# A state-space model inside a transformer layer: its elementwise passes on GpSimd, small corner clears on VectorE, its stores and loads one step earlier

## The chip, the cores and the metric

The kernel runs on one core of one Trainium2 chip. The metric is the device time of one execution in microseconds, the median of the runs shown. The core has five engines with an instruction stream each: TensorE (PE, with its weight loads shown as PEld), VectorE (DVE), ScalarE (ACT), GpSimd (POOL) and SyncE (SP), which here only issues DMA transfers (SPq in the trace). An engine takes its instructions strictly in the order in which they stand in its stream; where one waits, those behind it wait too.

## The reference

One layer of a hybrid encoder, for a prompt of 1024 frames and a running stream of 32 further frames (1056 columns together), in float32:

```python
proj = x @ w_in                                   # columns for attention, SSM and RWKV
mla_out  = mla_mixer(q_lat, kv_lat, k_rope, ...)  # 6 heads, causal in chunks of 64
s5_out   = s5_mixer(u, x0, ...)                   # 16 groups x 16 channels, 64 complex states each
rwkv_out = rwkv_mixer(p_rwkv, ...)                # 6 heads x 64
x = layer_norm(ALPHA * x + concat(mla_out, s5_out, rwkv_out) @ w_out)
x = layer_norm(ALPHA * x + square(relu(x @ w_up)) @ w_down)
```

The attention masks by chunks, and so on the diagonal of a block of 128 keys by 128 queries one corner of 64 by 64 is zero:

```python
key_chunk = arange(s) // 64
mask = key_chunk[None, :] <= q_chunk[:, None]
p = softmax(where(mask, s, NEG_INF)); out = p @ v
```

The SSM is a complex diagonal recurrence per group, and a gated output:

```python
state_t = lam_bar * state_(t-1) + b_bar @ u_t     # complex, 64 states per group
y = real(c @ state) + d * u
z = gelu(y);  s5_out = z * sigmoid(z @ w_glu + b_glu)
```

## The kernel before

The program passes four stages: projections and the set-up of RWKV (to about 320 us), the mix stage with attention, SSM and RWKV side by side (to about 700 us), the output projection with the first layer norm (to about 760 us), and the MLP. The change touches the mix stage alone.

**Order.** Three Python generators issue that stage. `stage_mix` advances attention, and after its 50th step, at every seventh, the SSM by one step (`S5_FROM`, `S5_STEP`); `side_by_side` sets 2.5 of these steps against one step of the RWKV stream. This gives the order in which the code is issued. A list scheduler then sets the order on each engine by its own costs of the instructions, so a row that becomes cheaper, dearer or ready earlier in its reckoning can move on every engine. `issue_after(mark)` keeps what it encloses behind an instruction named, for the SSM's steps behind the last VectorE instruction of the RWKV stream (`g.scan_dve`).

**The SSM, `stage_s5`.** The 16 groups go in four passes `q` of four. What follows calls them the first to the fourth group. A group holds one tile `ces` of 128 x 4 x 536 (two planes of tables, then the planes `e` and `es`), with the 64 real and 64 imaginary parts of the state on the 128 partitions. Its steps, each ended by a `yield`:

- SP loads the inputs and the kernel matrix (`ut`) and the input matrix `em`, and the tables (`ces<-tab_d`). PE multiplies (`s5e`), ACT copies into `e` and, with the halves swapped, into `es`, for two groups a step.
- L643 and L644: both planes times the tables, then added. ACT fills `es` with the decay (L645, `ces<-rho`), POOL clears two columns of it (L646), VectorE scans along the row (L647, the recurrence), and ACT writes the scan's halves swapped into `es` (L649, two of 64 x 536).
- L651 and L652: both planes times the tables, then subtracted.
- PE multiplies out (`s5y`), ACT copies (`yo`, inside `ces`), two groups a step; after them SP stores `z_d` (L665).

`ut`, `em` and `ces` have one buffer each, so the next group's loads wait until the last one's readers are done. Behind the fourth group stand the final states (`so`, L672 and L673), sixteen loads of the whole result (`zt<-z_d`, L680) and the Gelu on ACT (L683), with a load of its function table before it and one back to the exponentials behind it.

**Attention, `attn_out`.** For each tile of 128 keys PE makes scores `st`, ACT the numerators `ptk` (L1280, an exponential), POOL clears the corner on the diagonal (L1282), and PE multiplies with the values (`av`, L1255). At the end of a block of queries ACT copies the sums (`po`) and inverts them (L1263, L1264), and VectorE finishes (L1265 to L1268: `rt`, `rec`, `ot`). Row maxima are taken on VectorE (L1226, `mx<-sc`).

**RWKV.** Of its block steps, the pieces named later are: `ld`, the loads; PE's products `pra` and its transposes `prt` with ACT's copy `r` (L841); `prb`; the products `prn` with ACT's copy into `r` (L869); `prw` with ACT's copies `wu` (L883); `prg`; `pru` with ACT's copies `yb` (L919) and VectorE's `gq` (L917); and the chain over the state, `pry` and `prs` on PE (L940, L944) and `st` on VectorE (L946, L947), where each step needs the last. All these products share three banks of PSUM (`pr`).

Of the kernel before, what the change touches and what calls it, by code (L numbers as in the profile page):

```python
# [11 lines left out]
ALU = mybir.AluOpType  # L12
# [61 lines left out]
def log_exp_table(g, users, keep=True):  # L74

    pre = g.nc.scalar.preload_act_table_set("natural_log_exp_and_others")
    for u in users:
        g.tc.add_manual_dep(pre.ins, u.ins.name, mybir.DependencyInfo(mybir.DependencyClass.NoSync, mybir.DependencyReason.DATA), reason="table")
    if keep:
        g.le = pre.ins  # L80
# [318 lines left out]
G5 = 16  # L399
# [7 lines left out]
def bc(ap, shape):  # L407
    return ap.broadcast_to(shape)
# [191 lines left out]
NG = 4  # L600
# [3 lines left out]
def stage_s5(g):  # L604

    nc = g.nc
    V = nc.vector
    sp = g.s5  # L610
    for q in range(G5 // NG):
        gs = slice(NG * q, NG * q + NG)
        ut = sp.tile([P, NY * L5], F32, tag="ut", name="ut", bufs=1)
        u = ut[:, :NG * NY].rearrange("p (g k) -> p g k", k=NY)
        tz = ut[:, NG * NY:NG * NY + NG * P].rearrange("p (g x) -> p g x", x=P)
        nc.gpsimd.memset(u[:, :, P:P + 1], 0.0)
        nc.gpsimd.memset(tz, 0.0)
        src = g.u_d[q // 2][64 * (q % 2):64 * (q % 2) + 64].rearrange("(g c) (t k) -> (c t) g k", c=16, t=L5)
        nc.sync.dma_start(out=u[:, :, 0:P], in_=src[:, :, 0:P])
        nc.sync.dma_start(out=u[:, :, P + 1:NY], in_=src[:, :, P:NC5])  # L620
        em = sp.tile([P, NG, P], F32, tag="em", name="em", bufs=1)
        nc.sync.dma_start(out=em, in_=g.em_d[:, gs])
        for s in range(8):
            nc.sync.dma_start(out=tz[s:P:L5, :, 16 * s:P], in_=g.kt_d[:, gs, 0:(8 - s) * 16])
        ces = g.rl.tile([P, 4, NG * NX], F32, tag="ces", name="ces", bufs=1)
        tb = ces.rearrange("p w (g k) -> p w g k", k=NX)
        e, es = tb[:, 2], tb[:, 3]
        nc.sync.dma_start(out=tb[:, 0:2], in_=g.tab_d[:, :, gs])

        for j in range(0, NG, 2):  # L630
            ps = g.psc.tile([P, 512], F32, tag="sc", name="s5e")[:, :2 * NY].rearrange("p (j k) -> p j k", k=NY)
            for i in range(2):
                nc.tensor.matmul(out=ps[:, i], lhsT=em[:, j + i], rhs=u[:, j + i], start=True, stop=True)
            nc.scalar.activation(out=e[:, j:j + 2, 1:NX], in_=ps, func=AF.Copy)
            for i in range(2):
                nc.scalar.activation(out=es[hsl(1 - i), j:j + 2, 1:NX], in_=ps[hsl(i)], func=AF.Copy)
            yield
        nc.gpsimd.memset(tb[:, 2:4, :, 0:1], 0.0)
        nc.gpsimd.tensor_copy(out=e[:, :, P + 1], in_=g.x0[:, 0, gs])
        cl = sp.tile([P, NG, P], F32, tag="em", name="cl", bufs=1)  # L640
        nc.sync.dma_start(out=cl, in_=g.cl_d[:, P * NG * q:P * NG * (q + 1)].rearrange("p (g x) -> p g x", x=P))

        V.tensor_tensor(out=ces[:, 2:4], in0=ces[:, 2:4], in1=ces[:, 0:2], op=ALU.mult)  # L643
        V.tensor_tensor(out=ces[:, 2], in0=ces[:, 2], in1=ces[:, 3], op=ALU.add)  # L644
        nc.scalar.activation(out=es, in_=bc(g.rho[:, gs, None], [P, NG, NX]), func=AF.Copy)  # L645
        nc.gpsimd.memset(es[:, :, 0:P + 2:P + 1], 0.0)  # L646
        V.tensor_tensor_scan(out=ces[:, 2], data0=ces[:, 3], data1=ces[:, 2], initial=0.0, op0=ALU.mult, op1=ALU.add)  # L647
        for i in range(2):
            nc.scalar.activation(out=ces[hsl(1 - i), 3], in_=ces[hsl(i), 2], func=AF.Copy)  # L649
        yield  # L650
        V.tensor_tensor(out=ces[:, 2:4], in0=ces[:, 2:4], in1=ces[:, 0:2], op=ALU.mult)  # L651
        V.tensor_tensor(out=ces[:, 2], in0=ces[:, 2], in1=ces[:, 3], op=ALU.subtract)  # L652
        yield
        for i, k in enumerate((P, NX - 1)):
            nc.gpsimd.tensor_copy(out=g.fin[:, i, gs], in_=e[:, :, k])

        yo = ces[:, 3, :NG * NY].rearrange("p (g k) -> p g k", k=NY)
        for j in range(0, NG, 2):
            ps = g.psc.tile([P, 512], F32, tag="sc", name="s5y")[:, :2 * NY].rearrange("p (j k) -> p j k", k=NY)
            for i in range(j, j + 2):  # L660
                nc.tensor.matmul(out=ps[:, i - j], lhsT=tz[:, i], rhs=u[:, i], start=True, stop=False)
                nc.tensor.matmul(out=ps[:, i - j], lhsT=cl[:, i], rhs=e[:, i, 0:NY], start=False, stop=True)
            nc.scalar.activation(out=yo[:, j:j + 2], in_=ps, func=AF.Copy)
            yield
        nc.sync.dma_start(out=g.z_d[gs].rearrange("g x k -> x g k"), in_=yo)  # L665

    so = sp.tile([P, NG, P], F32, tag="em", name="so", bufs=1).rearrange("p a b -> p (a b)")[0:G5, 0:256].rearrange("p (i s r) -> p i s r", i=2, r=2)
    ps = g.psc.tile([P, 4, P], F32, tag="sc", name="s5l")
    for i in range(2):
        nc.tensor.transpose(out=ps[0:16, i], in_=g.fin[:, i], identity=g.ident)  # L670
    for i in range(2):
        nc.scalar.activation(out=so[:, i], in_=ps[0:16, i].rearrange("p (r s) -> p s r", r=2), func=AF.Copy)  # L672
        nc.scalar.dma_start(out=g.o["s5_p" if i == 0 else "s5_s"], in_=so[:, i])  # L673
    yield

    zt = g.rl.tile([P, 4, NG * NX], F32, tag="ces", name="zt", bufs=1).rearrange("p a b -> p (a b)")[:, :2 * L5 * NY]
    zv = zt.rearrange("p (h t k) -> p h t k", h=2, t=L5)
    for h in range(2):
        for i in range(8):
            nc.sync.dma_start(out=zv[16 * i:16 * i + 16, h], in_=g.z_d[8 * h + i].rearrange("(t c) k -> c t k", c=16))  # L680
    wg = sp.tile([P, NG, P], F32, tag="em", name="wg", bufs=1).rearrange("p a b -> p (a b)").rearrange("p (k m) -> p k m", k=2)
    nc.sync.dma_start(out=wg, in_=g.a["w_glu"])
    log_exp_table(g, [nc.scalar.activation(out=zt, in_=zt, func=AF.Gelu_apprx_tanh)], False)  # L683
    yield
    yield
    for m in range(2):
        om = sp.tile([P, NY * L5], F32, tag="ut", name="ot", bufs=1)
        ot = om.rearrange("p (k t) -> p t k", t=L5)
        for t, n in ((0, 3), (3, 3), (6, 2)):
            ps = g.psc.tile([P, 512], F32, tag="sc", name="s5g")[:, :n * NY]  # L690
            for k in range(2):
                nc.tensor.matmul(out=ps, lhsT=wg[:, k, m * P:m * P + P], rhs=zt[:, (k * L5 + t) * NY:(k * L5 + t + n) * NY], start=k == 0, stop=k == 1)
            nc.scalar.activation(out=ot[:, t:t + n], in_=ps.rearrange("p (t k) -> p t k", k=NY), func=AF.Identity, bias=g.vec[:, V_BGLU + m:V_BGLU + m + 1])
            yield
        log_exp_table(g, [nc.scalar.activation(out=om, in_=om, func=AF.Sigmoid)], False)
        V.tensor_tensor(out=ot, in0=ot, in1=zv[:, m], op=ALU.mult)
        nc.sync.dma_start(out=g.mg_d[3 + m, :, 0:TP], in_=om[:, 0:TP])
        nc.sync.dma_start(out=g.mg_d[3 + m, :, TP:T], in_=om[:, TP + L5:TP + L5 + TS])
        yield
# [13 lines left out]
def hsl(i):  # L713
    return slice(64 * i, 64 * i + 64)
# [527 lines left out]
def attn_out(g, h, qh, ql, vo, ot):  # L1242

    nc = g.nc
# [27 lines left out]
    for s, n in ((0, 512), (TP, TS), (512, 512)):  # L1272
        tiles = range((s + n) // P) if n > TS else range(8, 13)
        for kt in tiles:
            c = max(0, kt * P - s) if n > TS else 0
            w = P if kt < 12 else TS
            ps = g.pst.tile([P, 512], F32, tag="st", name="st")
            mm3(nc, [ps[:w, c:n]], kh[:, kt * P:kt * P + w], kl[:, kt * P:kt * P + w], [(qh[:, s + c:s + n], ql[:, s + c:s + n])], True, True)
            pt = g.ap.tile([P, 512], F32, tag="ptk", name="ptk", bufs=g.npt)
            nc.scalar.activation(out=pt[:w, c:n], in_=ps[:w, c:n], func=AF.Exp, scale=MLA_SCALE)  # L1280
            if n > TS and kt * P >= s:
                nc.gpsimd.memset(pt[64:128, c:c + 64], 0.0)  # L1282
            yield
            if late:
                av(*late)
                yield
            late = s, n, kt, c, w, pt, tiles
# [583 lines left out]
```

## Time and profile before

| What | Value |
|---|---|
| Median of 3 runs | 1610.53 us (1609.14 to 1616.11) |
| The profiled execution | 1609.9 us, span 1608.1 us |
| Mean granted TensorE clock | 0.965 |
| Share of the span: PE, DVE, ACT, POOL | 93%, 57%, 32%, 26% |

The span runs from the first instruction to the last; what lies outside it belongs to the execution's time. Rows of the profile name an instruction by line, engine, operation and tile (output <- input). A row of one stretch begins with its bounds and its width in us, then has for PE, PEld, DVE, ACT and POOL in turn the busy time and in brackets the number of instructions, then the granted clock (1 is full speed), the DMA engines' busy share and GB/s. A row of one instruction begins with its start and its duration, both in us; "x16" at its end means that so many stand together, and a bracket says how long the engine stood still just before and for what. A row of waits has the total in us, the number of waits and the longest.

### The profile page before, as it was taken

The page shows a single profiled execution, that of the slowest core. Times are in us where ns is not written, and L with a number is a line of the kernel's source. Part 1 is how long each engine was busy: PE and PEld are TensorE (multiplying, and loading weights), DVE is VectorE, ACT ScalarE, POOL GpSimd, SP SyncE. Part 2 cuts the span into 40 slices and gives each one's busy share as a digit, 9 for nine tenths or more (in the row PEclk, how much of TensorE's full clock was granted, in tenths as well). Part 3 has the DMA queues.
Part 4 walks back from the last instruction along what each step waited for, and adds up shares of the span by engine and source line. Part 5 has one row for each costly group of instructions (what it writes and reads, how often), then busy time and mean ns, then how long its engine had stood idle before and what let it go on. Part 6 is the DMA issues. An engine that isn't in the chain of part 4 may idle for free. (4 is left out here: it accounts for less than half of the span.)

```text
span 1608.1 us, 26358 instructions
## 1 busy us (share of the span) xinstructions
PE 1487.7 (93%) x10855; PEld 1336.1 (83%) x10855; DVE 920.6 (57%) x1676; ACT 510.6 (32%) x991; POOL 415.9 (26%) x394
## 2 busy tenths in 40 slices
PE   7899898578899798888999999999999999999995
PEld 7889786466667566566879999999999999999995
DVE  8476959363566544453865755554454454545457
ACT  5344433314544545542323212222121112221122
POOL 4623663511121101211422221222121112221123
PEclk9999999788999999999999999999999999999998
DMA  5314471437233221233512111111111111111012
GB/s 183 132 59 175 148 191 31 115 87 127 71 86 87 63 75 42 72 98 92 174 56 79 40 40 41 52 53 49 44 43 50 40 40 53 53 40 53 14 41 82
DMA packets 112621, 123.50 MB, mean 77 GB/s; under 512 B 51280, under 2 KB 87812, under 8 KB 112120
## 3 DMA queue, kind: packets, MB, share of 16 engines
q1 hardware_dynamic: 92516, 102.53, 21.8%
q10 hardware_dynamic: 19632, 18.27, 3.8%
q8 instruction: 85, 1.39, 0.4%
q0 software_dynamic: 352, 1.01, 0.2%
q14 instruction: 36, 0.29, 0.1%
HBM read 89.05 MB, written 32.68 MB: 76 GB/s over the span
## 5 line engine op out<-in xcount | busy, mean ns | idle before, releaser
L63 PE MATMUL acc<-xh,uphi 128*128 128x384 f32 (+1 forms) x768 | 249.0, 324 | 0.0
L65 PE MATMUL acc<-xl,uphi 128*128 128x384 f32 (+1 forms) x768 | 248.1, 323 | 0.0
L67 PE MATMUL acc<-xh,uplo 128*128 128x384 f32 (+1 forms) x768 | 247.8, 323 | 0.0
L1538 DVE TENSOR_TENSOR rl<-rl 128x384 f32<-128x384 f32 (+1 forms) x96 | 142.2, 1481 | 176.2 <-ACT rl L1537 174.3
L1566 DVE TENSOR_TENSOR yacc<-yacc,acc 128x384 f32<-128x384 f32 (+2 forms) x344 | 158.9, 508 | 112.1 <-PE acc L67 112.0
L63 PE MATMUL acc<-hh,dnhi 128*128 128x384 f32 (+2 forms) x736 | 209.3, 320 | 0.0
L65 PE MATMUL acc<-hl,dnhi 128*128 128x384 f32 (+2 forms) x736 | 207.2, 320 | 0.0
L67 PE MATMUL acc<-hh,dnlo 128*128 128x384 f32 (+2 forms) x736 | 197.5, 319 | 0.0
L50 POOL TENSOR_TENSOR dnlo<-dnraw,dnhi 128x1024 fp32r<-128x1024 f32 x30 | 72.5, 2417 | 336.8 <-ACT dnhi L49 321.5
L63 PEld LDWEIGHTS acc<-xh,uphi 128*128 128x128 f32 x768 | 144.2, 188 | 0.2 <-ACT xh L49 0.2
L65 PEld LDWEIGHTS acc<-xl,uphi 128*128 128x128 f32 x768 | 144.3, 188 | 0.0
L67 PEld LDWEIGHTS acc<-xh,uplo 128*128 128x128 f32 x768 | 144.3, 188 | 0.0
L50 POOL TENSOR_TENSOR uplo<-upraw,uphi 128x1024 fp32r<-128x1024 f32 x34 | 81.6, 2401 | 238.3 <-ACT uphi L49 238.3
L63 PE MATMUL acc<-xh,wmhi 128*128 128x384 f32 (+3 forms) x384 | 131.9, 344 | 9.3 <-ACT xh L49 8.2
L65 PE MATMUL acc<-xl,wmhi 128*128 128x384 f32 (+3 forms) x384 | 130.2, 339 | 1.6 <-DVE xl L50 1.6
L63 PEld LDWEIGHTS acc<-hh,dnhi 128*128 128x128 f32 x736 | 131.6, 188 | 0.0
L65 PEld LDWEIGHTS acc<-hl,dnhi 128*128 128x128 f32 x736 | 131.5, 188 | 0.0
L67 PE MATMUL acc<-xh,wmlo 128*128 128x384 f32 (+3 forms) x384 | 129.6, 338 | 0.0
L67 PEld LDWEIGHTS acc<-hh,dnlo 128*128 128x128 f32 x736 | 128.9, 188 | 0.0
L49 ACT ACTIVATE dnhi<-dnraw 128x1024 fp32r<-128x1024 f32 x30 | 31.8, 1060 | 298.9 <-PE acc L65 249.2
L49 ACT ACTIVATE hh<-rl 128x384 fp32r<-128x384 f32 (+1 forms) x96 | 47.9, 499 | 148.7 <-DVE rl L1538 148.7
L63 PEld LDWEIGHTS acc<-xh,wmhi 128*128 128x128 f32 (+1 forms) x384 | 73.9, 192 | 12.8 <-ACT xh L49 8.5
(489 smaller groups left out, 2881.2 us busy)
## 6 DMA issues: line engine op xcount, KB each, us to landing
upraw<-in_w_up SPq DMA_DIRECT2D x32, 512.0 KB
dnraw<-in_w_dn SPq DMA_DIRECT2D x30, 512.0 KB
ld<-rw SPq DMA_DIRECT2D x24, 320.0 KB
wmraw<-in_w_m SPq DMA_DIRECT2D x12, 512.0 KB
wo<-in_w_out SPq DMA_DIRECT2D x8, 512.0 KB
z<-in_xa SPq DMA_DIRECT2D x8, 512.0 KB
out_y<-o SPq DMA_DIRECT2D x8, 512.0 KB
xr<-in_xt SPq DMA_DIRECT2D x8, 384.0 KB
```

What stands on the lines that cost most here:

```text
L49: nc.scalar.activation(out=hi, in_=ps, func=AF.Copy)
L50: (lo_eng or nc.vector).tensor_tensor(out=lo, in0=ps, in1=hi.bitcast(F32), op=ALU.subtract)
L63: nc.tensor.matmul(out=outs[i], lhsT=lh, rhs=rhs[i][0], start=start, stop=False)
L65: nc.tensor.matmul(out=outs[i], lhsT=lh, rhs=rhs[i][1], start=False, stop=False)
L67: nc.tensor.matmul(out=outs[i], lhsT=ll, rhs=rhs[i][0], start=False, stop=stop)
L1538: nc.vector.tensor_tensor(out=r[:, :n], in0=r[:, :n], in1=r[:, :n], op=ALU.mult)
L1566: nc.vector.tensor_tensor(out=y, in0=y, in1=ps[i][:, :n], op=ALU.add)
```

## The change

It has three parts. The line numbers of the mix stage grow by 5 to 8: L643 becomes L648, L645 L650, L649 L654, L651 L656, L665 L670, L683 L691, L841 L849, L1280 L1288.

- The four elementwise passes of each group, sixteen in all, go from VectorE to POOL. The scan stays on VectorE, the copies on ACT.
- The 48 clears of the numerators' corners go from POOL to VectorE.
- `z_d`'s store and the next group's loads of `ut` and `em` are issued in the step of the last output copy, where they were issued at the beginning of the next step. The load of the tables stays where it was.

```diff
@@ -608,7 +608,8 @@
     nc = g.nc
     V = nc.vector
     sp = g.s5
-    for q in range(G5 // NG):
+
+    def load(q):
         gs = slice(NG * q, NG * q + NG)
         ut = sp.tile([P, NY * L5], F32, tag="ut", name="ut", bufs=1)
         u = ut[:, :NG * NY].rearrange("p (g k) -> p g k", k=NY)
@@ -622,6 +623,10 @@
         nc.sync.dma_start(out=em, in_=g.em_d[:, gs])
         for s in range(8):
             nc.sync.dma_start(out=tz[s:P:L5, :, 16 * s:P], in_=g.kt_d[:, gs, 0:(8 - s) * 16])
+        return gs, ut, u, tz, em
+
+    gs, ut, u, tz, em = load(0)
+    for q in range(G5 // NG):
         ces = g.rl.tile([P, 4, NG * NX], F32, tag="ces", name="ces", bufs=1)
         tb = ces.rearrange("p w (g k) -> p w g k", k=NX)
         e, es = tb[:, 2], tb[:, 3]
@@ -640,16 +645,16 @@
         cl = sp.tile([P, NG, P], F32, tag="em", name="cl", bufs=1)
         nc.sync.dma_start(out=cl, in_=g.cl_d[:, P * NG * q:P * NG * (q + 1)].rearrange("p (g x) -> p g x", x=P))
 
-        V.tensor_tensor(out=ces[:, 2:4], in0=ces[:, 2:4], in1=ces[:, 0:2], op=ALU.mult)
-        V.tensor_tensor(out=ces[:, 2], in0=ces[:, 2], in1=ces[:, 3], op=ALU.add)
+        nc.gpsimd.tensor_tensor(out=ces[:, 2:4], in0=ces[:, 2:4], in1=ces[:, 0:2], op=ALU.mult)
+        nc.gpsimd.tensor_tensor(out=ces[:, 2], in0=ces[:, 2], in1=ces[:, 3], op=ALU.add)
         nc.scalar.activation(out=es, in_=bc(g.rho[:, gs, None], [P, NG, NX]), func=AF.Copy)
         nc.gpsimd.memset(es[:, :, 0:P + 2:P + 1], 0.0)
         V.tensor_tensor_scan(out=ces[:, 2], data0=ces[:, 3], data1=ces[:, 2], initial=0.0, op0=ALU.mult, op1=ALU.add)
         for i in range(2):
             nc.scalar.activation(out=ces[hsl(1 - i), 3], in_=ces[hsl(i), 2], func=AF.Copy)
         yield
-        V.tensor_tensor(out=ces[:, 2:4], in0=ces[:, 2:4], in1=ces[:, 0:2], op=ALU.mult)
-        V.tensor_tensor(out=ces[:, 2], in0=ces[:, 2], in1=ces[:, 3], op=ALU.subtract)
+        nc.gpsimd.tensor_tensor(out=ces[:, 2:4], in0=ces[:, 2:4], in1=ces[:, 0:2], op=ALU.mult)
+        nc.gpsimd.tensor_tensor(out=ces[:, 2], in0=ces[:, 2], in1=ces[:, 3], op=ALU.subtract)
         yield
         for i, k in enumerate((P, NX - 1)):
             nc.gpsimd.tensor_copy(out=g.fin[:, i, gs], in_=e[:, :, k])
@@ -661,8 +666,11 @@
                 nc.tensor.matmul(out=ps[:, i - j], lhsT=tz[:, i], rhs=u[:, i], start=True, stop=False)
                 nc.tensor.matmul(out=ps[:, i - j], lhsT=cl[:, i], rhs=e[:, i, 0:NY], start=False, stop=True)
             nc.scalar.activation(out=yo[:, j:j + 2], in_=ps, func=AF.Copy)
+            if j:
+                nc.sync.dma_start(out=g.z_d[gs].rearrange("g x k -> x g k"), in_=yo)
+                if q < G5 // NG - 1:
+                    gs, ut, u, tz, em = load(q + 1)
             yield
-        nc.sync.dma_start(out=g.z_d[gs].rearrange("g x k -> x g k"), in_=yo)
 
     so = sp.tile([P, NG, P], F32, tag="em", name="so", bufs=1).rearrange("p a b -> p (a b)")[0:G5, 0:256].rearrange("p (i s r) -> p i s r", i=2, r=2)
     ps = g.psc.tile([P, 4, P], F32, tag="sc", name="s5l")
@@ -1279,7 +1287,7 @@
             pt = g.ap.tile([P, 512], F32, tag="ptk", name="ptk", bufs=g.npt)
             nc.scalar.activation(out=pt[:w, c:n], in_=ps[:w, c:n], func=AF.Exp, scale=MLA_SCALE)
             if n > TS and kt * P >= s:
-                nc.gpsimd.memset(pt[64:128, c:c + 64], 0.0)
+                nc.vector.memset(pt[64:128, c:c + 64], 0.0)
             yield
             if late:
                 av(*late)
```

The scheduler's order changes in few places. PE's order is the same but for the third group's `s5y`, which stands earlier; on SP the stores `z_d` and the loads `zt` keep their places, and loads of `ut` and `em` for the third and fourth group move ahead of some loads of attention and RWKV. Three places are shown.

ACT at the end of the SSM, before; RWKV's `sq` (the square in its norm) and the two `wu` stand just ahead of this piece, and L76 is the table load behind the Gelu:

```order
L672 ACTIVATE so<-s5l 16x128 x2
L673 DMA out_s_p<-so 16x128
L673 DMA out_s_s<-so 16x128
L1280 ACTIVATE ptk<-st 128x512
L1260 ACTIVATE po<-av 128x32
L1263 ACTIVATE rec<-po 64x32
L1264 ACTIVATE rec<-rec 64x32
L841 ACTIVATE r<-prt 128x512
L1280 ACTIVATE ptk<-st 128x512
L683 ACT_TABLE_LOAD
L683 ACTIVATE zt<-zt 128x2128
L76 ACT_TABLE_LOAD
```

ACT at the same place after the change:

```order
L980 ACTIVATE sq<-yc 128x384
L691 ACT_TABLE_LOAD
L691 ACTIVATE zt<-zt 128x2128
L76 ACT_TABLE_LOAD
L891 ACTIVATE wu<-prw 128x512
L891 ACTIVATE wu<-prw 128x256
L680 ACTIVATE so<-s5l 16x128 x2
L681 DMA out_s_p<-so 16x128
L681 DMA out_s_s<-so 16x128
L1288 ACTIVATE ptk<-st 128x512
```

The Gelu (`zt<-zt`) with its table loads has moved ahead of `wu`, `so` and a `ptk`, where it stood behind them and behind another block's `po`, `rec` and `r`.

ACT in the second group, before, from RWKV's `yb` on:

```order
L919 ACTIVATE yb<-pru 128x3x64 x2
L869 ACTIVATE r<-prn 128x3x128
L1280 ACTIVATE ptk<-st 128x512
L1260 ACTIVATE po<-av 128x32
L645 ACTIVATE ces<-rho 128x536
L1263 ACTIVATE rec<-po 64x32
L1264 ACTIVATE rec<-rec 64x32
L649 ACTIVATE ces<-ces 64x536 x2
L1280 ACTIVATE ptk<-st 128x512 x2
```

ACT there after the change:

```order
L927 ACTIVATE yb<-pru 128x3x64
L650 ACTIVATE ces<-rho 128x536
L654 ACTIVATE ces<-ces 64x536 x2
L877 ACTIVATE r<-prn 128x3x128
L1288 ACTIVATE ptk<-st 128x512
L1268 ACTIVATE po<-av 128x32
L1271 ACTIVATE rec<-po 64x32
L1272 ACTIVATE rec<-rec 64x32
L1288 ACTIVATE ptk<-st 128x512 x2
```

The decay's copy (`ces<-rho`) and the two half swaps (`ces<-ces`) now stand ahead of RWKV's `r<-prn`, of `ptk` and of `po`.

DVE at the same place, before; the row `SCALAR_TENSOR_TENSOR ces<-ces` (L647, L652 after the change) is the scan:

```order
L917 TENSOR_TENSOR gq<-pru,pc 128x192 x2
L643 TENSOR_TENSOR ces<-ces 128x1072
L1226 TENSOR_REDUCE mx<-sc 128x1
L644 TENSOR_TENSOR ces<-ces 128x536
L1265 COPY rt<-po 64x32
L946 TENSOR_TENSOR st<-prs,pc 128x192
L647 SCALAR_TENSOR_TENSOR ces<-ces 128x536
L947 TENSOR_TENSOR st<-st,gq 128x192
L1266 TENSOR_TENSOR rt<-rt,rec 64x32
```

DVE there after the change:

```order
L925 TENSOR_TENSOR gq<-pru,pc 128x192 x2
L1234 TENSOR_REDUCE mx<-sc 128x1
L652 SCALAR_TENSOR_TENSOR ces<-ces 128x536
L1273 COPY rt<-po 64x32
L1274 TENSOR_TENSOR rt<-rt,rec 64x32
L1275 SCALAR_TENSOR_TENSOR rec<-rt,rec 64x32
L1276 SCALAR_TENSOR_TENSOR ot<-po,rec 64x32
L954 TENSOR_TENSOR st<-prs,pc 128x192
L955 TENSOR_TENSOR st<-st,gq 128x192
L1233 MEMSET sc 64x64
L1234 TENSOR_REDUCE mx<-sc 128x1
```

The two passes are gone from it, and the scan stands ahead of the whole of `rt`, `rec` and `ot`, with the state update `st` behind these; before, the scan stood between the two halves of `st`, with `rt` around it.

## The prediction

> **What bounds the kernel now.** I read the page first, then busy time by stage, then PE's waits in the stage that is changed, then that stage in order of time at the places where the order of instructions moves.
>
> ```profile
> PE 1487.7 (93%) x10855; PEld 1336.1 (83%) x10855; DVE 920.6 (57%) x1676; ACT 510.6 (32%) x991; POOL 415.9 (26%) x394
> ```
> ```profile
> 380.00:590.00 210.00, 187.98 (x2014) 141.42 (x2013) 118.91 (x269) 104.39 (x230) 27.41 (x72) 0.96 0.31 79
> ...
> 760.00:1608.00 848.00, 827.53 (x5136) 808.25 (x5136) 474.02 (x775) 189.25 (x360) 193.68 (x97) 0.99 0.18 55
> ```
> PE (first pair after the width) is the bound. From 760 us on it is busy for 97.6%, so whatever the stage before gains or loses arrives at the end nearly whole. The SSM runs inside the first of these rows; there PE is busy for 188 of 210 us, so 22 us is all that waits could give back. The change keeps PE's work and, but for one group's output products, PE's order. So its price is what PE waits for:
>
> ```profile
> PE av L1255 <- POOL ptk L1282: 9.6, 7, 4.2
> ...
> PE prb L846 <- ACT r L841: 3.8, 1, 3.8
> ...
> PE sc L63 <- ACT ces L636: 2.4, 1, 2.4
> ...
> PE prg L897 <- DVE bn L858: 1.1, 1, 1.1
> PE s5e L633 <- DMA em<-em_d: 1.0, 1, 1.0
> ```
> Total us, times, longest. No wait of PE names an elementwise pass of the SSM directly: that chain runs beside PE, and only what queues behind it on DVE or ACT counts.
>
> **Gains.** The corners go from POOL to DVE, 48 small memsets:
>
> ```profile
> 405.18 0.27 ACT L1280 ACTIVATE ptk<-st 128x128 f32<-128x128 f32 x1
> 672.12 0.39 ACT L1280 ACTIVATE ptk<-st 128x256 f32<-128x256 f32 x1
> ```
> ```profile
> 406.99 0.80 PE L1255 MATMUL av<-ptk,vo 128*128 128x128 f32 x2 [2.49 <-POOL ptk L1282]
> 673.46 1.22 PE L1255 MATMUL av<-ptk,vo 128*128 128x256 f32 x2 [4.25 <-POOL ptk L1282]
> ```
> ```profile
> L1225 DVE MEMSET sc<- x48: 112/112/112, 324.9 to 649.4; 64x64 f32 x48
> ```
> ACT has written the block at 405.45 and 672.51, and an idle DVE would clear it 0.11 us later; PE goes on 1.54 and 0.95 us after ACT. With about 0.2 us of handover left, 1.3 and 0.8 us belong to POOL's queue, 2.1 of 6.7 us. A third of 9.6 is 3 us (0 to 9.6). The 48 x 0.112 = 5.4 us on DVE is covered by the passes that leave it:
>
> ```profile
> L643 DVE TENSOR_TENSOR ces<-ces x4: 1260/1266/1695, 396.7 to 545.2; 128x1072 f32<-128x1072 f32 x4
> L644 DVE TENSOR_TENSOR ces<-ces x4: 697/717/741, 398.0 to 547.2; 128x536 f32<-128x536 f32 x4
> ...
> L647 DVE TENSOR_TENSOR_SCAN ces<-ces x4: 1265/1274/1275, 399.7 to 548.9; 128x536 f32<-128x536 f32 x4
> ```
> Two such pairs per group, four groups: 8 x 1.98 = 15.9 us leave DVE. Where a pass stood ahead of what PE waits for (prg's wait on bn) 1.1 us goes; elsewhere DVE had room, 0. If the corners queued behind a waiting DVE instruction instead, this cover is gone and up to 1 us comes back. Loads and stores a step ahead: in SP's order they move only for the third and fourth groups, past max-row and gate loads that have several us of room; the em wait (1.0 us) goes, the 2.4 us wait hangs on a store whose place does not move, 0 (bounds 0 to 3.4). Gains: 3 + 1.1 + 1 = 5.1 us.
>
> **Cost 1: the Gelu.** At the end of the SSM, ACT's order now has the Gelu ahead of wu, so, ptk and r. When its input arrives does not change, since SP's order there is the same:
>
> ```profile
> 569.48 1.35 SPq L665 DMA_DIRECT2D z_d<-ces  x1
> 574.08 8.54 SPq L680 DMA_DIRECT2D zt<-z_d  x16
> ```
> ```profile
> 574.21 0.52 ACT L972 ACTIVATE sq<-yc 128x384 f32<-128x384 f32 x1 [1.27 <-DVE yc L970]
> 574.64 0.87 ACT L883 ACTIVATE wu<-prw 128x512 f32<-128x512 f32 x2
> ...
> 579.09 0.60 ACT L1280 ACTIVATE ptk<-st 128x512 f32<-128x512 f32 x1 [3.28 <-DMA zt<-z_d]
> ...
> 584.76 1.28 ACT L683 ACT_TABLE_LOAD   x1 [3.35 <-DMA zt<-z_d]
> ...
> 589.34 0.60 ACT L841 ACTIVATE r<-prt 128x512 f32<-128x512 f32 x1
> ```
> ```profile
> 576.12 1.16 PE L833 MATMUL pra<-ld 64*64 64x128 f32 x24
> ...
> 580.18 1.02 PE L1255 MATMUL av<-ptk,vo 128*128 128x512 f32 x2
> ...
> 589.99 0.56 PE L846 MATMUL prb<-ld 64*64 64x64 f32 x12 [3.78 <-ACT r L841]
> ```
> The store follows the last y copy, and sixteen loads take 8.5 us of SP's issue. Before, ACT did its other work and waited 3.35 us; Gelu with two table loads then held it to 589.34, and PE lost 3.78. Now ACT stands from 574.7 to 584.8, wu starts at 589.3 instead of 574.6, 14.7 us late, and ptk as much. PE's second half of pra (from 576.7) reuses the bank that wu frees, and its av at 580.18 needs that ptk: PE is some 14.5 us late there. The old 3.78 us does not come again, and about 1.2 us of slow clock that followed it is then shared: 9.5 us net. Bounds: 0, if the loads were in by then, and 14.7 - 3.8 = 10.9, if nothing is shared.
>
> **Cost 2: the second group's rho copy.** The order now puts rho and the two half swaps ahead of r, ptk and po on ACT, and the scan ahead of rt to ot and the state update st on DVE.
>
> ```profile
> 442.44 0.19 POOL L639 COPY ces<-x 128x4 f32<-128x4 f32 x1
> ```
> ```profile
> 443.03 0.59 ACT L919 ACTIVATE yb<-pru 128x192 f32<-128x192 f32 x2
> 444.48 0.49 ACT L869 ACTIVATE r<-prn 128x384 f32<-128x384 f32 x1 [0.86 <-PE prn L868]
> ...
> 446.23 0.65 ACT L645 ACTIVATE ces<-rho 128x536 f32<-128x536 f32 x1
> ...
> 448.39 1.31 ACT L649 ACTIVATE ces<-ces 64x536 f32<-64x536 f32 x2 [1.13 <-DVE ces L647]
> ```
> ```profile
> 446.78 0.36 DVE L946 TENSOR_TENSOR st<-prs,pc 128x192 f32<-128x192 f32 x1 [0.30 <-PE prs L944]
> ...
> 448.27 0.33 DVE L947 TENSOR_TENSOR st<-st,gq 128x192 f32<-128x192 f32 x1
> ```
> ```profile
> 448.66 0.56 PE L940 MATMUL pry<-gq,st 64*64 64x64 f32 x12 [0.51 <-DVE st L947]
> ```
> The passes on POOL are not in this trace; near sizes are:
>
> ```profile
> L238 POOL TENSOR_TENSOR mix<-raw 128x1058 f32<-128x1058 f32 x10 | 20.0, 1999 | 1.5 <-DMA rw<-mix 1.5
> ...
> L388 POOL TENSOR_TENSOR kk<-kk,at 128x1058 f32<-128x1058 f32 x3 | 9.9, 3291 | 9.0 <-DVE fc L342 5.5 <-DVE nn L342 3.4
> ...
> L344 POOL TENSOR_TENSOR mix<-mix,cs 128x1024 f32<-128x1024 f32 x3 | 7.6, 2520 | 0.0
> ```
> I take 2.5 us for 1072 columns (L344, a product like ours, nearest in kind; ends 2.0 and 3.3) and half that for 536. From 442.6 the pair ends at 446.4; ACT, free at 443.6, waits 2.8 us and copies rho to 447.0. A product r stands ahead of the small memset on POOL (about 1 us), so the scan runs 447.5 to 448.8 (1.27 us, L647), the swaps to 450.1, then r, ptk, po and two small passes to 451.8. Only then come rt to ot and st on DVE, ending about 453 instead of 448.6. PE's pry waits 4.3 us more, and a wait of that length costs clock too:
>
> ```profile
> 474.00:482.00 8.00, 5.79 (x44) 4.77 (x44) 5.25 (x15) 1.16 (x3) 2.60 (x3) 0.57 0.70 182
> ```
> That is the 2.4 us wait at 476: 8 us at a granted clock of 0.57, about 3 us lost beyond the wait. So 4.3 + 2.7 = 7 us; with 2.0 us passes the wait is 3.5, with 3.3 us ones 5.5, and without clock loss 3.5 is the low end; 0 if other slack takes it.
>
> **Cost 3.** In the fourth group the swaps stand between two key copies:
>
> ```profile
> 545.37 0.68 ACT L49 ACTIVATE kh<-sck 64x512 fp32r<-64x512 f32 x2 [1.66 <-PE sck L1119]
> ```
> ```profile
> 548.78 0.30 PE L63 MATMUL sc<-kh,qh 128*128 128x128 f32 x1 [2.49 <-DVE kl L50]
> ```
> The scan and 1.31 us of swaps put that copy from 545.4 to about 547.4, and two DVE passes less behind it give some back: 1.5 us (0 to 2). The first and third groups show ptk at most 1.5 us late on ACT with room for it: 0.
>
> **Sum.** -5.1 + 9.5 + 7 + 1.5 = 12.9 us; half a chance that the shorter wait at 407 keeps the clock up takes 1: 11.9. The profiled execution took 1609.9 us (span 1608.1 and 1.8 around it), the median of the runs is 1610.5: 1622 us.
>
> A page that speaks against the move: the Trainium skill (GPSIMD Engine Reference, the table of which engine to choose) says that two-input elementwise work runs about twice as slow there as on VectorE. The trace agrees: 2.0 to 2.5 against 1.27 us. By exactly twice, 2.53 us, the sum stays at 1622.
>
> **Rivals.**
> R1, the pure gain (the other side): the loads end before ACT reaches the Gelu and POOL's passes end before ACT reaches rho; cost 1 to 3 are 0. It decides if zt is complete by 574.7, 10 us earlier than now. Against it: SP issues 8.5 us of loads after a store that lands at 574.1. For it: nothing but slack that I misjudge. 1610.5 - 5.1 = 1605, with all the waits on POOL 1599. Chance 0.12.
> R2, one stall only: ACT's wait in the second group is absorbed (PE there runs 0.5 us from its own wait, so I doubt it) or the Gelu's, by half. 1610.5 + 12 - 7 = 1615. Chance 0.21.
> R3, POOL and DVE block each other: 16 passes of 1.25 to 2.5 us on POOL beside DVE's two-input passes. L388 at 3.29 against L238 at 2.0 and L643's longest at 1.70 against 1.27 show what meeting costs. If each of the eight long passes holds a DVE pass for 1 us that PE needs, 1622 + 8 = 1630. Chance 0.08; most DVE passes there are not waited for.
> The Trainium skill (SBUF — State Buffer, who interferes with whom) has the rule for it: a DVE instruction with two SBUF inputs and a GpSimd one that reads SBUF exclude each other for a whole instruction. The trace agrees in kind, with the two pairs of durations just named.
>
> **How the numbers follow.** My forecast, both stalls, has 0.59. About 0.5% (8 us) is what a measurement of this kernel can tell from no change: faster is under 1602.5, slower over 1618.6. R1 gives faster 0.08 and same 0.04; R2 same 0.19 and slower 0.02; the forecast slower 0.55 and same 0.04; R3 slower. Together 0.08, 0.27, 0.65. The range runs from 1607, which leaves out R1, to 1630, R3's time; the forecast alone spans 1616 to 1628.
>
> **What would show it.** On ACT: a wait of about 10 us on the zt loads ahead of the Gelu's table load, and PE idle 12 us or more soon after; a wait of 2 to 4 us on POOL ahead of the second rho copy, and PE's pry waiting about 5 us on st. On POOL: passes of 2.0 to 3.3 us. PE's waits on corners down to some 6 us, now on DVE or ACT. I am wrong if the ACT waits are there and PE stays busy, or if the loads of zt start earlier against the last y copy than 5.4 us.

## The result and the profile after

| | Before | After |
|---|---|---|
| Median | 1610.55 us (4 runs, 1609.14 to 1616.11) | 1635.39 us (4 runs, 1633.44 to 1636.34) |
| Ratio, with its 95% interval | 1 | 1.0139 (1.0106 to 1.0172) |
| Span of the profiled execution, mean clock | 1608.1 us, 0.965 | 1633.7 us, 0.957 |
| Forecast | | 1622 us, range 1607 to 1630 |

The change makes the kernel slower, as forecast, but by 25 us by the medians (1.39% or 22 us by the ratio) where 12 were forecast, and the time lies above the range. First the page of the changed kernel, then two stretches of it, each with its bounds and width, then busy time of PE, PEld, DVE, ACT and POOL, then clock:

```profile
PE 1493.3 (91%) x10855; PEld 1337.8 (82%) x10855; DVE 918.9 (56%) x1708; ACT 511.0 (31%) x991; POOL 439.1 (27%) x362
```
```profile
380.00:590.00 210.00, 179.38 (x1924) 135.69 (x1924) 109.97 (x264) 95.21 (x215) 54.12 (x64) 0.92 0.30 74
...
785.00:1633.00 848.00, 826.67 (x5136) 807.34 (x5136) 474.26 (x775) 189.16 (x360) 193.36 (x97) 0.99 0.18 55
```

The last 848 us hold the same 5136 matmuls as before, in the same busy time within 1 us: the MLP has passed the loss through, and all of it was made before. From 380 to 590 us POOL's busy time has doubled, from 27.4 to 54.1 us, and PE got through 90 matmuls fewer. PE's waits of the changed kernel between 320 and 760 us (total, times, longest) name the places:

```profile
PE pra L841 <- ACT wu L891: 12.6, 1, 12.6
PE pry L948 <- DVE st L955: 10.1, 5, 7.3
...
PE av L1263 <- DVE ptk L1290: 7.0, 7, 3.6
...
PE av L1263 <- ACT ptk L1288: 2.3, 1, 2.3
```

The two long waits are those of costs 1 and 2. The corners' 9.6 us became 7.0, now on VectorE. The 2.3 us on ScalarE are no wait for a corner: they stand at 722.56 us, ahead of a block of 32 x 32 of the stream, in which nothing is cleared, and whose `ptk` ScalarE makes behind a copy (`mh<-mraw`) that waited 5.19 us for its load; before, that `ptk` stood ahead of the copy. The Gelu's place, in order of time, SP's loads first:

```profile
583.25 7.84 SPq L688 DMA_DIRECT2D zt<-z_d  x16
```
```profile
583.55 0.52 ACT L980 ACTIVATE sq<-yc 128x384 f32<-128x384 f32 x1 [1.15 <-DVE yc L978]
593.71 1.28 ACT L691 ACT_TABLE_LOAD   x1 [9.63 <-DMA zt<-z_d]
...
598.29 0.87 ACT L891 ACTIVATE wu<-prw 128x512 f32<-128x512 f32 x2
```
```profile
598.94 1.54 PE L841 MATMUL pra<-ld 64*64 64x128 f32 x12 [12.61 <-ACT wu L891]
```
```profile
586.00:600.00 14.00, 1.40 (x18) 1.15 (x14) 0.68 (x2) 5.70 (x7) 0.00 (x0) 0.63 0.41 60
600.00:612.00 12.00, 12.00 (x59) 8.33 (x59) 3.30 (x10) 4.33 (x10) 0.00 (x0) 0.72 0.09 26
```

ScalarE stands for 9.63 us in front of the Gelu's table load, `wu` starts 14.74 us after `sq` (0.43 before), and PE waits 12.61 us; in the 12 us behind it PE is busy throughout at a granted clock of 0.72. The second group:

```profile
442.09 2.49 POOL L648 TENSOR_TENSOR ces<-ces 128x1072 f32<-128x1072 f32 x1
...
446.01 0.65 ACT L650 ACTIVATE ces<-rho 128x536 f32<-128x536 f32 x1 [2.94 <-POOL ces L649]
...
448.34 1.31 ACT L654 ACTIVATE ces<-ces 64x536 f32<-64x536 f32 x2 [1.67 <-DVE ces L652]
...
449.72 2.44 POOL L656 TENSOR_TENSOR ces<-ces 128x1072 f32<-128x1072 f32 x1 [0.80 <-ACT ces L654]
...
450.61 1.59 DVE L1273 COPY rt<-po 64x32 f32<-64x32 f32 x1 [2.31 <-ACT po L1268]
...
452.24 1.31 POOL L657 TENSOR_TENSOR ces<-ces 128x536 f32<-128x536 f32 x1
452.31 1.29 DVE L1274 TENSOR_TENSOR rt<-rt,rec 64x32 f32<-64x32 f32 x1
...
454.50 0.36 DVE L955 TENSOR_TENSOR st<-st,gq 128x192 f32<-128x192 f32 x1
...
454.91 0.91 PE L948 MATMUL pry<-gq,st 64*64 64x64 f32 x12 [7.33 <-DVE st L955]
```

Two rows were not foreseen: a copy and a product of 64 x 32 elements on VectorE take 1.59 and 1.29 us, and each ends when the POOL pass beside it ends (452.20 beside 452.16, 453.60 beside 453.55).

Below, "matmul by matmul" means that the start of the same matmul is compared in the traces of two kernels, each counted from its span's start. So read, the loss stands at few places:

| Place, in the times of the kernel before | Changed kernel against it, us (+ is lost) | Forecast, us |
|---|---|---|
| from the start to 446 us | -0.6 | -1 (the clock at 407) |
| 446 to 456, the second group | +9.2 | +7 |
| 456 to 505, the third group | +1.2 | 0 |
| 505 to 526, where the waits of `prg` on `bn` and of `s5e` on `em` stood | -3.7 | -2.1 |
| 526 to 574, the fourth group | +3.3 | +1.5 |
| 574 to 600, the Gelu | +10.8 | +9.5 |
| 600 to 760 | +5.4 | 0 |
| all | +25.6 | 11.9, with -3 for the corners, which wait at several places |

### The profile page after: what moved, and what is told of

Its sections match the earlier page's. It is cut to its first block, busy times and chain, and to the rows that moved or that the text cites. A ratio compares the mean times of both kernels' runs of the same rounds, so it can differ in the third digit from the quotient of the medians.

```text
span 1633.7 us, 26308 instructions
## 1 busy us (share of the span) xinstructions
PE 1493.3 (91%) x10855; PEld 1337.8 (82%) x10855; DVE 918.9 (56%) x1708; ACT 511.0 (31%) x991; POOL 439.1 (27%) x362
## 3 DMA queue, kind: packets, MB, share of 16 engines
q8 instruction: 85, 1.39, 0.4%
## 5 line engine op out<-in xcount | busy, mean ns | idle before, releaser
L1263 PE MATMUL av<-ptk,vo 128*128 128x512 f32 (+5 forms) x204 | 77.2, 462 | 9.3 <-DVE ptk L1290 7.0
```

The costliest lines, as they stand in the source:

```text
L1263: nc.tensor.matmul(out=po[:, c:n], lhsT=vo[:w, kt].rearrange("p a x -> p (a x)")[:, 64 * i:64 * i + P], rhs=pt[:w, c:n], start=kt == tiles ...
```

## The experiments

All times below are medians with the ratio to the kernel before, run on the same chip in the same session; its own medians there were 1609.9 to 1611.1 us. Executions of one kernel scatter by 10 to 18 us here, so an interval of a ratio is 0.3 to 0.6% wide, and a difference of two kernels under some 5 us is not told apart.

| Kernel | Median, us | Ratio (95% interval) |
|---|---|---|
| corners_only | 1619.02 | 1.0053 (1.0033 to 1.0073) |
| passes_only | 1624.93 | 1.0091 (1.0067 to 1.0114) |
| loads_only | 1610.12 | 1.0002 (0.9981 to 1.0023) |
| gelu_held | 1621.33 | 1.0069 (1.0041 to 1.0096) |
| both_held | 1612.61 | 1.0008 (0.9991 to 1.0026) |
| second_group_held | 1608.65 | 0.9986 (0.9966 to 1.0006) |
| before_gelu_held | 1605.91 | 0.9963 (0.9943 to 0.9983) |
| corners_held | 1610.38 | 0.9994 (0.9974 to 1.0013) |
| corners_second_held | 1606.97 | 0.9982 (0.9960 to 1.0004) |
| passes_gelu_held | 1613.14 | 1.0003 (0.9979 to 1.0028) |
| pieces | 1623.70 | 1.0078 (1.0053 to 1.0104) |
| stores_on_pool | 1605.04 | 0.9974 (0.9954 to 0.9994) |

### One part at a time

**corners_only**, against the kernel before:

```diff
-                nc.gpsimd.memset(pt[64:128, c:c + 64], 0.0)
+                nc.vector.memset(pt[64:128, c:c + 64], 0.0)
```

> Only the 48 corner clears move to VectorE; passes, store and loads stand as before. If the corners bring what the prediction said (their queue on POOL is what PE waits for), 3 us faster: 1607.5, and PE's waits on corners fall from 9.6 to some 6 us. If, as the trace of the whole change suggests (9.3 us of such waits on VectorE and ScalarE), the clear waits on VectorE for as long, 1610.5 within 2 us. In both theories the Gelu stands behind the other work on ScalarE as before, and no stall of 10 us is seen.

Measured: 1619.02, slower than either theory. PE's waits on corners did fall as forecast, but the second group was stalled with the passes still on VectorE, since this edit too makes the scheduler put the decay's copy ahead of `r<-prn`. Its waits between 320 and 760 us, and the second group in order of time:

```profile
PE av L1255 <- DVE ptk L1282: 6.6, 5, 3.2
...
PE pry L940 <- DVE st L947: 6.2, 4, 4.2
```
```profile
445.95 0.65 ACT L645 ACTIVATE ces<-rho 128x536 f32<-128x536 f32 x1 [2.61 <-DVE ces L644]
...
450.01 0.17 DVE L1265 COPY rt<-po 64x32 f32<-64x32 f32 x1 [1.94 <-ACT po L1260]
...
450.53 0.19 DVE L1266 TENSOR_TENSOR rt<-rt,rec 64x32 f32<-64x32 f32 x1 [0.35 <-ACT rec L1264]
...
452.00 0.91 PE L940 MATMUL pry<-gq,st 64*64 64x64 f32 x12 [4.16 <-DVE st L947]
```

This is a control for the changed kernel. The decay's copy starts at 445.95 here and at 446.01 there, where PE stands 0.3 us ahead of here, so POOL's slower pair delayed it by 0.3 us at most. The same small copy and product take 0.17 and 0.19 us with no pass on POOL beside them. PE's wait is 4.16 instead of 7.33 us, and of the 3.2 us between them 1.42 + 1.10 = 2.5 are these two rows.

**passes_only**, against the kernel before (four lines of this kind):

```diff
-        V.tensor_tensor(out=ces[:, 2:4], in0=ces[:, 2:4], in1=ces[:, 0:2], op=ALU.mult)
+        nc.gpsimd.tensor_tensor(out=ces[:, 2:4], in0=ces[:, 2:4], in1=ces[:, 0:2], op=ALU.mult)
```

> Only the sixteen passes move to POOL; corners, store and loads stand as before. In its order of instructions the Gelu stands behind wu and so, but ahead of the next numerators (ptk) and of po; the decay's copy of the second group stands behind r, ptk and po as before. Theory 1 (ScalarE's order makes the loss): the second group's 9 us do not appear, and of the Gelu's 11 us those that hang on ptk alone remain, 5 to 10: 1616 to 1621. Theory 2 (passes on POOL hold VectorE wherever they run, whatever the order): the loss is spread and stays near the whole 25 us: 1630 or more.

Measured: 1624.93, between the two theories. Its waits between 320 and 760 us:

```profile
PE av L1255 <- POOL ptk L1282: 10.2, 7, 4.0
PE av L1255 <- ACT po L1260: 9.7, 1, 9.7
```

The Gelu's stall is there, now through `po`; the second group's is not, PE's longest wait on `st` being 1.4 us. Theory 1 is right on both; the few us above its range fit what passes_gelu_held shows below.

**loads_only**, with `load(q)` and the store's place as in the change and nothing else:

```diff
+            if j:
+                nc.sync.dma_start(out=g.z_d[gs].rearrange("g x k -> x g k"), in_=yo)
+                if q < G5 // NG - 1:
+                    gs, ut, u, tz, em = load(q + 1)
             yield
-        nc.sync.dma_start(out=g.z_d[gs].rearrange("g x k -> x g k"), in_=yo)
```

> Only the store and the next group's loads are issued a step earlier; passes and corners stand as before. Prediction's term: the 1.0 us wait on em goes, 1609.5. Rival: loads ahead of other loads on SyncE cost a wait elsewhere, 1612 to 1614. Both say that it is not what makes 25 us.

Measured: 1610.12, no difference; the 1 us of the prediction can't be told here.

### The order on ScalarE

**gelu_held**, against the changed kernel:

```diff
-    log_exp_table(g, [nc.scalar.activation(out=zt, in_=zt, func=AF.Gelu_apprx_tanh)], False)
-    yield
+    yield
+    with g.tc.issue_after(last_traced(g, mybir.EngineType.Activation)):
+        log_exp_table(g, [nc.scalar.activation(out=zt, in_=zt, func=AF.Gelu_apprx_tanh)], False)
     yield
```

> The whole change, but the Gelu is issued one step later and held behind ScalarE's instructions that were issued by then, so that wu, so, ptk, po and two r stand ahead of it. Theory 1 (the Gelu's place makes the loss of 575 to 596 us): PE's wait of 12.6 us on wu goes, and 11 us with it: 1624. Rival (the loads come late anyway and the stall moves with the Gelu to the next copy behind it): 1631 or more, with a wait of 5 to 10 us on r or ptk behind the Gelu.

Measured: 1621.33, and PE's wait on `wu` is gone. PE's waits from 570 to 606 us:

```profile
PE av L1264 <- ACT po L1269: 2.4, 1, 2.4
PE pry L949 <- DVE st L956: 0.4, 1, 0.4
```

By the medians the Gelu's place costs 14 us of the changed kernel, by the ratios 0.70% or 11 us.

**before_gelu_held**: the same edit on the kernel before.

> The kernel before, with the Gelu held as in gelu_held and nothing else changed. By the Gelu's place alone: before has 3.8 us of waiting on r behind the Gelu, which go: 1607. Rival (the loads of zt end so late that whatever stands behind the Gelu waits): 1610 or more.

Measured: 1605.91, faster than the kernel before by 0.37% (0.17 to 0.57%), since the 3.8 us wait on `r` and the slow clock behind it go. So of the 11 to 14 us some 4 to 6 were already paid before, and 5 to 10 are the change's. Matmul by matmul, the kernel before pays 6.0 us at that place, which before_gelu_held doesn't; the changed kernel loses 16.8 us there against the kernel before and gets 6.0 of it back, 10.8 net. This is more than the difference of the times, since gelu_held has a loss of its own at that place, 4.2 us, behind a store that ScalarE issues (more on it under stores_on_pool).

**both_held**: gelu_held, and in each group

```diff
-        nc.scalar.activation(out=es, in_=bc(g.rho[:, gs, None], [P, NG, NX]), func=AF.Copy)
+        yield
+        with g.tc.issue_after(last_traced(g, mybir.EngineType.Activation)):
+            nc.scalar.activation(out=es, in_=bc(g.rho[:, gs, None], [P, NG, NX]), func=AF.Copy)
...
             nc.scalar.activation(out=ces[hsl(1 - i), 3], in_=ces[hsl(i), 2], func=AF.Copy)
-        yield
```

> The whole change, with the Gelu held as in gelu_held and the decay's copy, the scan and the half swaps of each group issued a step later and held on ScalarE behind what was issued by then, so that RWKV's r, ptk and po go first. Theory 1 (ScalarE's order makes the loss): the second group's 9 us go too, 1621 - 9 = 1612, and PE's longest wait on st falls from 7.3 us to under 2. Rival (POOL's passes hold VectorE wherever they run): still 1618 or more, with VectorE's two-input passes of 1.2 to 2.4 us ahead of st or of a clear.

Measured: 1612.61, theory 1's value within 1 us, and PE's longest wait on `st` is 1.4 us. All three parts of the change are in this kernel, sixteen passes on POOL among them, and the loss is gone. But the later copy costs something in the first group, where PE's matmuls fall 5.6 us behind those of gelu_held between 382 and 422 us, and so **second_group_held** has this edit `if q == 1` alone.

> The whole change with the Gelu held, and the decay's copy held a step later in the second group alone; the other three groups keep the whole change's order. Theory 1 (the second group's order costs 9 to 12 us; in both_held the first group's later copy gave 4 us of that back): 1621 - 11 = 1610, 2 to 5 us under both_held. Rival (POOL's passes hold VectorE in all groups, and both_held only hid it): 1613 or more.

Measured: 1608.65, as theory 1 said. The second group's stall is thus worth 12.7 us by the medians or 0.83%, 13 us, by the ratios, with some 5 us of uncertainty on either side; matmul by matmul, gelu_held loses 9.1 us there. PE's rows show 6.0 us more of waiting than here (7.33 for 1.35), and slow clock behind it. Where `pry` waited 7.33 us, this kernel has

```profile
445.77 0.56 PE L953 MATMUL pry<-gq,st 64*64 64x64 f32 x12 [1.35 <-DVE st L960]
```

### What POOL's passes and the corners cost by themselves

**pieces**, against the changed kernel, all sixteen passes so:

```diff
-        nc.gpsimd.tensor_tensor(out=ces[:, 2], in0=ces[:, 2], in1=ces[:, 3], op=ALU.subtract)
+        for k in range(0, 536, 134):
+            nc.gpsimd.tensor_tensor(out=ces[:, 2, k:k + 134], in0=ces[:, 2, k:k + 134], in1=ces[:, 3, k:k + 134], op=ALU.subtract)
```

> The whole change, with each of the sixteen passes on POOL cut into four pieces of columns (four times 268 or 134 a plane). ScalarE's and VectorE's order in the second group is the same as in the whole change. Theory 1 (POOL holds VectorE for one whole instruction): rt's copy and product there, 1.59 and 1.29 us in the whole change, fall to at most 0.2 plus a piece, some 0.8 and 0.6 us, and PE's wait on st falls by 1 to 2 us unless the pieces make the decay's copy later by as much. Rival (the two engines share bandwidth, or the copy is slow for another reason): both stay at 1.2 us or more. The time as a whole tells little here, since the Gelu stands behind wu in this order: 1625 to 1636.

Measured, in the second group (the order there is that of the changed kernel):

```profile
447.83 2.88 POOL L659 TENSOR_TENSOR ces<-ces 128x268 f32<-128x268 f32 x4 [0.80 <-ACT ces L656]
...
448.72 0.60 DVE L1277 COPY rt<-po 64x32 f32<-64x32 f32 x1 [2.31 <-ACT po L1272]
...
449.43 0.63 DVE L1278 TENSOR_TENSOR rt<-rt,rec 64x32 f32<-64x32 f32 x1
...
450.09 0.67 DVE L1279 SCALAR_TENSOR_TENSOR rec<-rt,rec 64x32 f32<-64x32 f32 x1
```

The hold shrinks with POOL's instruction: 0.60 and 0.63 us, one piece, where whole passes made 1.59 and 1.29. So it is one engine excluding the other for a whole instruction, and not a shared rate. PE gains nothing from it, since four pieces take 2.88 us for 2.44, the decay's copy waits 3.67 us for 2.94, and a third small row is held too: PE waits 7.3 us as before. The whole took 1623.70, a ratio of 1.0078 for the changed kernel's 1.0139 and 1 us under what was expected. That is no gain in the second group, where PE loses 8.9 us for 9.2 matmul by matmul. The Gelu stands behind `wu` in this order and costs 6.7 us for 10.8, and behind 600 us nothing is lost.

**passes_gelu_held**: passes_only with the Gelu held.

> Only the sixteen passes on POOL, with the Gelu held; corners, store and loads as before. It is to before_gelu_held (1605.9) what the passes are with the two stalls on ScalarE absent. If passes on POOL cost only through the order on ScalarE: 1606 within 2. If they hold VectorE ahead of what PE waits for (st in the third group, the split keys in the fourth): 1609 to 1612. If their being off VectorE is a gain by itself: 1603 or less.

Measured: 1613.14, against 1605.91 for before_gelu_held; by the ratios 0.40% (about 6 us) more, with intervals of 0.20 and 0.25% on either side. So with both stalls on ScalarE absent the passes bring nothing and probably cost some us. Matmul by matmul, this kernel loses 7.4 us against before_gelu_held between 385 and 600 us, of which 1.9 stand at the Gelu's place behind ScalarE's store. In the third group, in the changed kernel, one place is seen at which a pass holds what PE waits for, a state update that takes 0.36 us in the second group (at 454.50, shown above) and here ends 0.23 us behind the pass:

```profile
497.02 2.48 POOL L648 TENSOR_TENSOR ces<-ces 128x1072 f32<-128x1072 f32 x1 [0.69 <-POOL ces L644]
...
498.14 1.59 DVE L955 TENSOR_TENSOR st<-st,gq 128x192 f32<-128x192 f32 x1
```

**corners_held** (both_held with passes, store and loads as before) and **corners_second_held** (the same with the hold in the second group alone):

> Corners on VectorE and the passes left on VectorE, store and loads as before, with the Gelu and the decay's copy held as in both_held. It is to both_held what the passes and loads are: where POOL's passes cost nothing once the order is held, it takes as long as both_held within 3 us; where they hold VectorE at a cost, it is 5 us or more faster. Against corners_only (1619), theory 1 (the second group's order made its loss) says 1608 to 1611, the rival (clears on VectorE wait in a longer queue) 1615 or more.

> Corners on VectorE, passes on VectorE, store and loads as before, the Gelu held, the decay's copy held a step later in the second group alone. It is to before_gelu_held (1605.9) what the corners are, once their change of order is taken out. The prediction's term says 3 us less: 1603; with no gain from the corners 1606; if clears wait behind VectorE's other work, 1609 or more.

Measured: 1610.38, 2 us under both_held, and 1606.97, against 1605.91 for before_gelu_held without the corners (and without the later copy, whose own price in this kernel no run shows). The corners' 3 us of waiting do not come out as time. One place shows why. The longest of these waits stands in the kernel before from 669 to 673.46 us. In corners_only it is 1.0 us shorter (3.23 for 4.25). PE's next rows there, of the kernel before and of corners_only:

```profile
673.26 0.23 POOL L1282 MEMSET ptk<- 64x64 f32 x2
...
680.43 0.50 PE L65 MATMUL st<-ql,kh 128*128 128x512 f32 x1 [0.73 <-DMA ql<-ml]
```
```profile
679.31 0.39 ACT L1280 ACTIVATE ptk<-st 128x256 f32<-128x256 f32 x1
679.77 0.11 DVE L1282 MEMSET ptk<- 64x64 f32 x1 [5.81 <-ACT ptk L1280]
679.93 0.70 PE L1255 MATMUL av<-ptk,vo 128*128 128x256 f32 x2 [3.23 <-DVE ptk L1282]
...
685.82 0.80 PE L63 MATMUL st<-qh,kh 128*128 128x512 f32 x1 [2.86 <-DMA qh<-mh]
...
687.28 0.79 PE L65 MATMUL st<-ql,kh 128*128 128x512 f32 x1 [0.67 <-DMA ql<-ml]
```

The numerators' block was written from 672.12 and from 679.31. The row `st<-ql,kh` starts 8.31 us later before and 7.97 us later here: PE arrives sooner and waits 2.86 us for the maxima (`qh<-mh`), and of 1.0 us won 0.3 are left.

### A version that beats both

**stores_on_pool**, against second_group_held. There ScalarE, having copied `so` by 571.67, could issue its store only at 577.53:

```diff
-        nc.scalar.dma_start(out=g.o["s5_p" if i == 0 else "s5_s"], in_=so[:, i])
+        nc.gpsimd.dma_start(out=g.o["s5_p" if i == 0 else "s5_s"], in_=so[:, i])
```

> second_group_held, with the two stores of the SSM's final states (out_s) issued by POOL's queue where ScalarE's issued them. In second_group_held ScalarE's issue of the first stands until 577.53, 5.9 us after so was copied, while SyncE issues the sixteen loads of zt; PE then waits 3.0 us on po. If that issue is what holds ScalarE, PE's wait on po goes and 3 to 5 us with it: 1604 to 1606, or by the ratio 0.995 to 0.997. Rival (ScalarE waits for something of the loads that any issue would meet, and PE is not short of it): 1608 within 2, with a wait as long elsewhere.

Measured: 1605.04, ratio 0.9974 (0.9954 to 0.9994), the time as expected and the ratio just above. PE's 3.0 us wait on `po` is gone from its list. By the times alone this kernel is not told apart from second_group_held (0.9986); matmul by matmul it loses 4.9 us less at the Gelu's place, and that is ScalarE's store. Both this kernel, with the whole change in it, and before_gelu_held, with none of it, are faster than the kernel before, and the two can't be told apart; matmul by matmul they gain 5.4 and 5.7 us on the kernel before between 385 and 600 us. What brings the time is the order on ScalarE.

## Why the prediction was wrong in size

No one term makes the miss of 13.7 us that the table by places shows: the corners' 3 us and the 5.4 us behind 600 us are the most of it, then the second and the fourth group with some 2 us each.

- **The Gelu, cost 1: right.** Forecast were a wait of about 10 us ahead of the table load and `wu` 14.7 us late; 9.63 and 14.3 us were measured, the store and loads kept their places, and the change's share is 5 to 10 us by the times and 10.8 us matmul by matmul for the 9.5 forecast. That the slow clock is shared fits, though its price was not measured apart.
- **The second group, cost 2: the chain right, the price too low.** POOL's passes took 2.48 and 1.32 us (2.5 and 1.25 forecast), ScalarE waited 2.94 us (2.8). The step that failed is "rt to ot and st on DVE, ending about 453": they ended at 454.86, because two 64 x 32 rows were held for 2.5 us by POOL's second pair. Against the kernel before, PE's wait grew by 6.8 us (7.33 for 0.51), not 4.3, and with the slow clock behind it the place costs more than the 7 us forecast: matmul by matmul, PE is 0.6 us ahead of the kernel before at 447.7 us and 8.6 us behind it at 451.6. The prediction blamed POOL's slowness for the late decay's copy; corners_only shows the copy as late, within 0.3 us, with VectorE's passes, because they start later and their own queue there (a row maximum between the two) takes its time too. What moved the copy was the corners' move.
- **The gains: the corners' -3 us did not come.** The small terms came: in the changed kernel PE no longer waits on `bn` ahead of `prg`, the wait on `em` fell from 1.0 to 0.3 us, and 3.7 us were won there for 2.1 forecast. The corners' waits fell too, by 3 us in corners_only, as forecast, and from 9.6 to 7.0 us in the changed kernel, but were handed on to the next wait: corners_second_held has no gain on before_gelu_held. From 600 us on, where the longest of these waits stands, the changed kernel loses 5.4 us instead; 2.3 us of waiting there are the block of 32 x 32 behind `mh<-mraw`. The rest stays open: over that stretch the other kernels' traces lie between 0.4 us won and 10.6 lost, and none isolates it. The prediction had asked what VectorE gets rid of, not what POOL's passes do to the rest of it.
- **The fourth group, cost 3: the place right, the price too low.** With the half swaps ahead of the key copy, as forecast, PE's wait on `kl` is 3.69 us for 2.49. Not forecast was that `ql` on VectorE takes 1.37 us for 0.72 beside one of POOL's passes, and that PE's wait ahead of `sck`, on a row of VectorE behind that one, grows from 1.13 to 1.86 us. Matmul by matmul 3.3 us are lost, for 1.5; no run isolates it.
- **R3 was priced as a rival that takes the forecast's place, 1630 with a chance of 0.08.** It happened beside the forecast: POOL's instructions did hold VectorE's, for 1.59 us where 0.17 was due, on top of the two stalls. In the changed kernel seven rows of VectorE were held by the sixteen passes, for 6 us in all beyond what they take elsewhere. The range ended at R3's time because nothing was added to it. The rule that the prediction took from the Trainium skill (SBUF — State Buffer, who interferes with whom) agrees with the trace: rows with two SBUF inputs are held until POOL's row ends. That section also counts VectorE's 2-port modes among the rows that are held, which fits the copy of one input; no run here shows which mode it ran in.

In sum, going from before_gelu_held over second_group_held and gelu_held to the changed kernel by the ratios: the rest 0.23%, the second group 0.83%, the Gelu 0.70%, less the 0.37% of it that the kernel before paid too, together 1.39%, or 22 us; forecast were 9.5, 7 and -4.6, 12 us. The 0.23% have 0.3% of uncertainty on either side, and ScalarE's store (4.9 us in second_group_held) can be all of it.

## What to carry to other kernels

Where a scheduler sets the order, compare the order of each one-part edit, since here the stall in the second group came with the harmless part (48 clears) and the one at the Gelu with the passes. An instruction that waits for a long chain of transfers belongs behind everything that is ready by then: holding the Gelu a step back made even the kernel before 0.37% faster. When work moves to an engine that shares a resource with another, add the holds to the other costs; they don't replace them.

## What the hardware showed that was not expected

- POOL's two-input pass held VectorE's small SBUF rows until it ended, many times as long as they take alone (1.59 us for 0.17 above), and not the rows that read PSUM. In the changed kernel's first group:

```profile
389.68 2.48 POOL L648 TENSOR_TENSOR ces<-ces 128x1072 f32<-128x1072 f32 x1 [0.70 <-ACT ces L641]
391.81 0.35 DVE L856 TENSOR_TENSOR r<-prb,msk 128x192 f32<-128x192 f32 x1
...
392.24 1.33 POOL L649 TENSOR_TENSOR ces<-ces 128x536 f32<-128x536 f32 x1
392.27 1.33 DVE L1239 TENSOR_TENSOR m<-mx 128x9 f32<-128x9 f32 x1
```

  The row that reads `prb` from PSUM takes its 0.35 us beside L648; the maximum of 128 x 9 (`m<-mx`, two inputs in SBUF) takes 1.33 us beside L649, where the kernel before has 0.17 us at 393.64.
- A store issued by ScalarE stood for 5.9 us while SyncE issued sixteen loads, and held all of ScalarE behind it; issued by POOL it held nothing that PE waits for. Why it stood was not tried.
